# A two-layer diffusion block on one core: seven block products for fourteen more pairs of weight tiles, and modulation steps in three feed-forwards

## The chip, the cores and the metric

The kernel runs on one core of a Trainium2 chip. The metric is the time of one execution on the device in microseconds, the median of several runs.

## The reference

Two layers work on 256 image tokens and 256 context tokens, each a row of 1024 values in float32. A layer is a feed-forward, a token mixer (neighbourhood attention and pooling) and a second feed-forward. In front of each stands an RMS norm with a modulation (shift and scale), behind each a second norm with a gate. The nine modulation vectors of a layer come from a product of a conditioning vector with a 1024 x 9216 matrix, once for the image and once for the context:

```python
def mod_vectors(cvec, w_mod, b_mod):
    m = jax.nn.silu(cvec) @ w_mod + b_mod
    return jnp.split(m, N_MOD, axis=-1)

def swiglu(h, w_gate_up, w_down):
    gate, up = jnp.split(h @ w_gate_up, 2, axis=-1)
    return (jax.nn.silu(gate) * up) @ w_down

def sandwich_ffn(x, w_gate_up, w_down, g_pre, g_post, shift, scale, gate):
    h = modulate(rms_norm(x, g_pre), shift, scale)
    return x + 0.5 * gate * rms_norm(swiglu(h, w_gate_up, w_down), g_post)
```

The hidden width of the feed-forward is 2816, that is 22 tiles of 128. The last layer yields the image tokens only: its vectors 5 to 8 are needed for the image alone, and its second feed-forward runs on 256 tokens.

## The kernel before

**Precision.** Every float32 operand of a matmul is split in a high part (rounded by ScalarE) and a low part (the difference, by VectorE), and `mm3` makes three matmuls of one product. So each weight tile costs ScalarE a copy and VectorE a subtraction ("prep") before TensorE can use it.

**A feed-forward** (`ffn`) goes through 22 pairs of tiles (gate and up) of the first weight. Per pair, `gate_up` makes 2 x 8 products of 512 columns, that is 48 matmuls, and `gate_up_evac` applies SiLU, multiplies and splits the result into G. The pairs form groups; behind each group but the last the down product of the group is made for all tokens in two column halves and added up in Y (copied by ScalarE in the first group, added by VectorE in the later ones). Behind the last group comes the rest of the down product token tile by token tile, and `close` applies norm, gate, residual, next norm and modulation, transposes the tile and splits it into the next input. The four token tiles are 0, 1 (image) and 2, 3 (context). The first pairs ("lead") run on one half of the tokens first, so that they can start before the last two token tiles are closed.

**Seven block products.** For pairs from `LEAD` on of feed-forward (1,0) (layer 1, first), gate and up together form a 2 x 2 block product: gate and up times two halves of the depth, tokens in two halves. `gate_up_seven` makes seven products of quarter size in place of eight: 7 x 4 x 3 = 84 matmuls of 256 columns. It needs sums of weight blocks (`prep_seven`: four GpSimd additions, three and a half weight tiles split) and sums of input blocks (`add_up`, eight additions on GpSimd and eight splits, once per feed-forward), and VectorE adds the products up from PSUM. Its input lies paired: token tiles in the order 2, 0, 3, 1, two and two. Feed-forwards with seven products use `S_GROUPS` (4, 4, 4, 4 and 6 pairs), the others `F_GROUPS` (8, 8 and 6).

**Modulation.** Two vectors of layer 0 are made first by TensorE. The other sixteen are made on VectorE, beside the feed-forwards: a step loads one 128 x 1024 block (`wm`, 512 KB) and multiplies and adds it into an accumulator of each stream (`acc`); after eight such steps a ninth gathers the accumulator with eight small DMAs per stream (`part`), three GpSimd additions, and a matmul with `sel`. These 16 x 9 = 144 steps stand in a list. `fill(n)` takes n more steps from it (fractions add up) after each pair; the rates are `RATE` for (0,0), `LATER` for (0,1), by group. `need` takes what is missing before a vector is read.

**Order of work.** Nothing is issued while the code above runs: a recorder takes the operations down, and `order` plans them by list scheduling, each engine taking the operation that can start first, then by recorded rank (`haste` moves some forward). Buffers come from pools with numbered places: 16 `big`, 2 `raw`, 10 `wk`, 8 PSUM banks. A weight stream (`Stream`) prepares one entry ahead of use. All instructions are issued from one line (387), so the profile's groups go by tile names: `pg`, `pu` gate and up, `p` the seven products, `pd` down, `pt` transposes, `w` and `wb` split weights, `s` sums of weight blocks, `ht` sums of input blocks, `g` and `tt` the pair's result, `c` and `u` the sums of products.

Of the kernel before, what the change touches and what calls it, by code (L numbers as in the profile page):

```python
# [22 lines left out]
NF = 22  # L23
# [3 lines left out]
AHEAD = 1  # L27
F_GROUPS = ((0, 8), (8, 16), (16, 22))
S_GROUPS = ((0, 4), (4, 8), (8, 12), (12, 16), (16, 22))
SEVEN = {(1, 0)}  # L30
NEXT_SEVEN = {(1, 0)}
ORDER = (2, 0, 3, 1)
PLAIN = {t: t for t in range(4)}
PAIRED = {t: i for i, t in enumerate(ORDER)}
# [1 line left out]
LEAD = 3  # L36
# [1 line left out]
BLOCK = 4  # L38
PLACES = {"big": 16, "raw": 2, "wk": 10, "ps": 8, "st": 24}
LIMITS = {"ps": 1}  # L40
RATE = (2.6, 2.6, 2.6)
LATER = (2.6, 4.2, 5.6)
NONE = (0.0,) * 5
BEHIND = 0
MARGIN = 6.0
# [5 lines left out]
XS, CS, ALL = slice(0, S), slice(S, N_TOK), slice(0, N_TOK)  # L51
# [353 lines left out]
def tile_dit_block(  # L405
# [30 lines left out]
    def bank(base="ps"):  # L436
        return rec.tile("ps", [P, 512], F32, base)
# [88 lines left out]
    ws = Stream()  # L526

    def plan_ffn(l, ff):
        groups = S_GROUPS if (l, ff) in SEVEN else F_GROUPS
        for gi, (f0, f1) in enumerate(groups):  # L530
            if l == DEPTH - 1 and ff == 1 and gi == 0:
                for k in range(0, KD, 2):
                    ws.add(wblock[k : k + 2].rearrange("k p c -> p k c"), 2)
                f0 += BLOCK
            for f in range(f0, f1):
                ws.add(wgu[l, ff, f], None, (l, ff) in SEVEN and f >= LEAD)
            f0 = groups[gi][0]
            if gi + 1 < len(groups):
                for h in range(2):
                    for f in range(f0, f1, 4):  # L540
                        ws.add(wdn[l, ff, f : f + 4, :, h * 512 : (h + 1) * 512].rearrange("f p c -> p f c"), 4)
            else:
                for f in range(f0, f1, 2):
                    ws.add(wdn[l, ff, f : f + 2].rearrange("f p c -> p f c"), 2)
# [171 lines left out]
    def fill(n):  # L716

        debt[0] += n
        rec.delay = BEHIND
        while debt[0] >= 1 and todo:  # L720
            steps = todo[0][1]
            steps.pop(0)()
            debt[0] -= 1
            if not steps:
                todo.pop(0)
        rec.delay = 0
# [7 lines left out]
    H = {}  # L734
# [63 lines left out]
    def new_h(paired=False):  # L798
        return Input(paired)
# [89 lines left out]
    def columns(o, w, cs):  # L889
        for k in range(KD):  # L890
            kk = slice(k * P, (k + 1) * P)
            hh = H["now"][k // 4]
            mm3(
                o[:, cs],
                (w[:, 0, kk], w[:, 1, kk]),
                (hh[0][:, k % 4, cs], hh[1][:, k % 4, cs]),
                k == 0,
                k == KD - 1,
            )

    def columns_half(o, w, half):
        for k in range(KD):
            kk = slice(k * P, (k + 1) * P)
            h = H["now"][k // 4][half]
            mm3(
                o[:, half * S : (half + 1) * S],
                (w[:, 0, kk], w[:, 1, kk]),
                (h[:, 0, k % 4, :], h[:, 1, k % 4, :]),
                k == 0,
                k == KD - 1,  # L910
            )
# [21 lines left out]
    def ffn(l, ff, both, nxt, rate, lead, parts):  # L933
        cs = ALL if both else XS
        N = N_TOK if both else S
        seven = (l, ff) in SEVEN
        at = PAIRED if seven else PLAIN
        groups = S_GROUPS if seven else F_GROUPS
        toks = (2, 3, 0, 1) if both else (0, 1)
# [3 lines left out]
        def lhs(f):  # L943
            g = G[f // 2]
            return g[:, f % 2, 0, :], g[:, f % 2, 1, :]
# [6 lines left out]
        def gate_up_evac(f, pg, pu):  # L952
            tt = wtile([P, 2, 512], "tt")
            product(tt[:, :, :N], pg[:, cs], pu[:, cs])
            if f % 2 == 0:
                G[f // 2] = slot([P, 2, 2, N_TOK], "g")
            hi, lo = lhs(f)
            split(hi[:, :N], lo[:, :N], tt[:, 0, :N])

        def gate_up(fs, parts):  # L960
            held = []
            for f in fs:
                held.append((f, ws.get(), ws.get(), bank("pg"), bank("pu")))
            for part in parts:
                for i, (f, wg, wup, pg, pu) in enumerate(held):
                    if seven and part is parts[1] and i == 1:
                        H["now"].add_up()
                    if seven:
                        columns_half(pg, wg, part)
                        columns_half(pu, wup, part)  # L970
                    else:
                        columns(pg, wg, part)
                        columns(pu, wup, part)
                    if part is parts[-1]:
                        gate_up_evac(f, pg, pu)
# [27 lines left out]
        def by_token():  # L1003

            wb = [ws.get() for _ in range(KD)]
            for q in range(BLOCK // 2):
                G[q] = slot([P, 2, 2, N_TOK], "g")
            for t in toks:
                tk = slice(t * P, (t + 1) * P)
                pg, pu = bank("pg"), bank("pu")  # L1010
                for k in range(KD):
                    hh = H["now"][k // 4]
                    for o, c in ((pg, HALVES[0]), (pu, HALVES[1])):
                        mm3(o, (hh[0][:, k % 4, tk], hh[1][:, k % 4, tk]), (wb[k][:, 0, c], wb[k][:, 1, c]), k == 0, k == KD - 1)
                tt = wtile([P, 2, 512], "tt")
                product(tt, pg, pu)
                pt = turn(tt[:, 0, :], 0)
                for q in range(BLOCK // 2):
                    src = pt[:, q * S : (q + 1) * S].rearrange("p (e c) -> p e c", e=2)
                    split(G[q][:, :, 0, tk], G[q][:, :, 1, tk], src)  # L1020

        for gi, (f0, f1) in enumerate(groups):
            f = f0
            if gi == 0 and parts is None:
                by_token()
                f = BLOCK
            elif gi == 0:
                gate_up(tuple(range(lead)), parts)
                f = lead
                fill(lead * rate[gi])  # L1030
            while f < f1:
                if seven:
                    gate_up_seven(f)
                else:
                    gate_up((f,), (cs,))
                f += 1
                fill(rate[gi])
            if gi + 1 < len(groups):
                for h in range(2):
                    hc = slice(h * 512, (h + 1) * 512)  # L1040
                    pd = {t: bank("pd") for t in toks}
                    for q in range(f0, f1, 2):
                        w = ws.get()
                        for i in range(2):
                            hi, lo = lhs(q + i)
                            for t in toks:
                                tk = slice(at[t] * P, (at[t] + 1) * P)
                                c = slice(i * 512, (i + 1) * 512)
                                mm3(
                                    pd[t], (hi[:, tk], lo[:, tk]), (w[:, 0, c], w[:, 1, c]),  # L1050
                                    q + i == f0, q + i == f1 - 1,
                                )
                    for t in toks:
                        if gi == 0:
                            if h == 0 and t % 2 == 0:
                                Y[t // 2] = slot([P, 2, D], "y", F32)
                            nc.scalar.activation(Y[t // 2][:, t % 2, hc], pd[t], AF.Copy)
                        else:
                            nc.vector.tensor_add(Y[t // 2][:, t % 2, hc], Y[t // 2][:, t % 2, hc], pd[t])
# [5 lines left out]
        f0, f1 = groups[-1]  # L1065
        paired = nxt is not None and nxt in NEXT_SEVEN
        toks = ORDER if paired else toks
# [8 lines left out]
        Hn = None  # L1076
        for t in toks:
# [3 lines left out]
            if Hn is None and nxt is not None:  # L1081
                Hn = new_h(paired)
# [4 lines left out]
    def token_mix(l, nxt):  # L1087
        full = l == 0
# [230 lines left out]
        for pr in range(4):  # L1319
            bx = wtile([P, 2, 6, 64], "bx")  # L1320
            nc.sync.dma_start(out=bx, in_=biasx[l, pr])
            now = qk
# [12 lines left out]
                    k_part(qk)  # L1335
                    q_part(qk)

        toks = (2, 3, 0, 1) if full else (0, 1)
        load_gate(l, 5, (0, 1) if full else (0,))
        need(*nxt)  # L1340
        need(nxt[0], nxt[1] + 1)
# [10 lines left out]
        Hn = None  # L1352
        for t in toks:
            if t not in pd:
                pd[t] = (bank("pd"), bank("pd"))
                sweep(pd[t], mixed, w4, t, True, False)
            sweep(pd[t], mixed, kept, t, False, True)
            if Hn is None:
                Hn = new_h()
            close(t, pd[t], None, False, nxt, Hn)  # L1360
        H["now"] = Hn

# [20 lines left out]

    ffn(0, 0, True, (0, 3), RATE, START, (CS, XS))
    token_mix(0, (0, 6))
    ffn(0, 1, True, (1, 0), LATER, LEAD, (CS, XS))
    ffn(1, 0, True, (1, 3), NONE, LEAD, (0, 1))
    token_mix(1, (1, 6))
    ffn(1, 1, False, None, NONE, 0, None)

# [105 lines left out]
```

## Time and profile before

| | us |
|---|---|
| median of 3 runs | 1657.71 |
| lowest and highest | 1657.25, 1659.05 |
| profiled execution | 1658.03 |
| its span, first to last instruction | 1656.0 |

From the matmuls in order of time, the stages of the profiled execution are:

| stage | starts, us |
|---|---|
| feed-forward (0,0) | 37.5 |
| token mixer 0 | 411.8 |
| feed-forward (0,1), pairs 0 to 7 | 603.7 |
| its first down product | 696.8 |
| pairs 8 to 15 | 740.9 |
| second down product | 830.8 |
| pairs 16 to 21 | 875.7 |
| last down product and closing | 943.0 |
| feed-forward (1,0) | 979.9 |
| its first seven-product pair | 1017.7 |
| token mixer 1 | 1328.8 |

Engines: PE is TensorE's matmuls, PEld its weight loads, DVE VectorE, ACT ScalarE, POOL GpSimd, SP the queue that issues the DMAs. A row of the stage view holds the stretch, its length, and the busy time of each engine with its instructions. A row of a tile's view holds the count and the least, median and greatest duration in ns. In a row in order of time, the bracket is the idle time before the instruction and what ended it.

### The profile page before, as it was taken

To read this page: it belongs to the slowest core of one execution; us is meant where nothing else is said; L and a number is where in the kernel's file an instruction comes from. 1 tells how busy PE (TensorE), PEld (TensorE's weight loads), DVE (VectorE), ACT (ScalarE), POOL (GpSimd) and SP (SyncE) were. 2 spreads that over 40 slices of the span, in tenths; PEclk is the share of its full clock that TensorE was granted. 3 is DMA by queue.
4 is the path that set the end of the run, shared out by engine and by line. 5 is a ranking of instruction groups with operands and counts; after the bars stand their busy time and mean duration, and the time that the engine had idled before them with its cause. 6 is when DMAs were issued, how large, how long until landed. Compare 5 with 4: busy or idle time off the path is not lost.

```text
span 1656.0 us, 23501 instructions
## 1 busy us (share of the span) xinstructions
PE 1613.0 (97%) x9074; PEld 1390.3 (84%) x9074; DVE 1212.7 (73%) x1662; ACT 736.6 (44%) x1292; POOL 356.9 (22%) x348
## 2 busy tenths in 40 slices
PE   6999999999999899999999999999999999899998
PEld 4988888888878689888888879999989888778997
DVE  7985766546689779867776488677788778875554
ACT  7522322225566663222222264534444567774442
POOL 1022011101131311110211036363463122210000
PEclk9999999999999999999999999999999999999999
DMA  9466556532221436666698412233233421355551
GB/s 376 185 230 243 209 194 225 175 118 83 86 78 65 157 108 223 235 204 230 211 351 300 159 52 96 83 103 127 77 116 114 144 90 70 132 200 199 196 200 55
DMA packets 98958, 269.09 MB, mean 162 GB/s; under 512 B 9424, under 2 KB 39328, under 8 KB 87072
## 3 DMA queue, kind: packets, MB, share of 16 engines
q1 hardware_dynamic: 98848, 267.60, 45.5%
q8 instruction: 71, 1.16, 0.3%
q14 instruction: 39, 0.32, 0.1%
HBM read 251.80 MB, written 1.09 MB: 153 GB/s over the span
## 4 chain that ended last, share of the span: by engine, by line
PE 84%; DVE 6%; ACT 5%; POOL 2%; issue 2%; DMA 1%; SPq 0%; POOLq 0%; DVEq 0%; ACTq 0%
PE pd_ps L387 26%; PE pu_ps L387 19%; PE pg_ps L387 19%; PE p_ps L387 11%; PE pv_ps L387 2%; ACT n_wk L387 2%; PE pk_ps L387 2%; POOL rs_st L387 2%; DVE w_big L387 1%; PE pq_ps L387 1%; DMA w_big<-in_wmod_dram 1%; PE pt_ps L387 1%; ACT sx_wk L387 1%; PE po_ps L387 1%; ACT w_big L387 1%
## 5 line engine op out<-in xcount | busy, mean ns | idle before, releaser
L387 DVE TENSOR_TENSOR w_big<-raw_raw,w_big 128x1024 fp32r<-128x1024 f32 x293 | 369.8, 1277 | 122.5 <-ACT w_big L387 122.2
L387 PE MATMUL pd_ps<-w_big,g_big 128*128 128x512 f32 x1848 | 430.7, 393 | 0.0
L387 PEld LDWEIGHTS pd_ps<-w_big,g_big 128*128 128x128 f32 x1848 | 345.7, 188 | 77.7 <-ACT grows L387 0.2
L387 ACT ACTIVATE w_big<-raw_raw 128x1024 fp32r<-128x1024 f32 x293 | 302.8, 1054 | 228.9 <-DMA raw_raw<-in_wgu_dram 94.6
L387 PE MATMUL pu_ps<-h_big,w_big 128*128 128x512 f32 (+1 forms) x1944 | 366.4, 341 | 0.0
L387 PEld LDWEIGHTS pu_ps<-h_big,w_big 128*128 128x128 f32 x1944 | 303.7, 188 | 42.5
L387 PE MATMUL pg_ps<-h_big,w_big 128*128 128x512 f32 (+1 forms) x1752 | 330.3, 342 | 1.4 <-ACT h_big L387 1.4
L387 PEld LDWEIGHTS pg_ps<-h_big,w_big 128*128 128x128 f32 x1752 | 275.6, 189 | 41.3 <-ACT h_big L387 1.8
L387 DVE SCALAR_TENSOR_TENSOR acc_wk<-wm_wk,csil,acc_wk 128x1024 f32<-128x1024 f32 x196 | 244.2, 1285 | 81.5 <-DMA wm_wk<-in_wmod_dram 81.2
L387 POOL TENSOR_TENSOR part_wk<-part_wk 128x512 f32<-128x512 f32 (+2 forms) x84 | 87.7, 1045 | 496.1 <-DMA part_wk<-acc_wk 418.5
L387 ACT ACTIVATE g_big<-tt_wk 128x512 fp32r<-128x512 f32 (+1 forms) x84 | 49.2, 586 | 275.6 <-DVE tt_wk L387 258.4
L387 POOL TENSOR_SCALAR rs_st<-sq_st 128x1 f32<-128x1 f32 x24 | 7.5, 312 | 448.8 <-ACT n_wk L387 448.7
L387 POOL TENSOR_TENSOR s_wk<-raw_raw 128x512 f32<-128x512 f32 x38 | 64.1, 1695 | 126.3 <-DMA raw_raw<-in_wgu_dram 120.5
L387 PE MATMUL p_ps<-h_big,w_big 128*128 128x256 f32 x684 | 86.8, 281 | 0.0
L387 PEld LDWEIGHTS p_ps<-h_big,w_big 128*128 128x128 f32 x684 | 83.5, 189 | 0.3
L387 PE MATMUL p_ps<-ht_big,w_big 128*128 128x256 f32 x684 | 82.9, 279 | 0.0
L387 PEld LDWEIGHTS p_ps<-ht_big,w_big 128*128 128x128 f32 x684 | 81.2, 189 | 0.0
L387 DVE TENSOR_TENSOR g_big<-tt_wk,g_big 128x512 fp32r<-128x512 f32 (+1 forms) x84 | 57.8, 688 | 29.3 <-ACT g_big L387 29.2
L387 PE MATMUL pd_ps<-w_big,mix_big 128*128 128x512 f32 x288 | 71.6, 397 | 0.5 <-DVE mix_big L387 0.5
L387 DVE TENSOR_TENSOR w_big<-s_wk,w_big 128x1024 fp32r<-128x1024 f32 x38 | 59.0, 1554 | 15.2 <-ACT w_big L387 15.2
L387 ACT ACTIVATE tt_wk<-pg_ps 128x512 f32<-128x512 f32 (+1 forms) x67 | 35.7, 533 | 75.9 <-PE pg_ps L387 65.8
L387 DVE TENSOR_TENSOR y_big<-y_big,pd_ps 128x512 f32<-128x512 f32 x72 | 48.4, 685 | 27.0 <-PE pd_ps L387 27.0
(157 smaller groups left out, 1771.7 us busy)
## 6 DMA issues: line engine op xcount, KB each, us to landing
raw_raw<-in_wgu_dram SPq DMA_DIRECT2D x84, 1024.0 KB, 4.9
wm_wk<-in_wmod_dram SPq DMA_DIRECT2D x128, 512.0 KB, 6.8
raw_raw<-in_wdn_dram SPq DMA_DIRECT2D x44, 1024.0 KB, 5.2
part_wk<-acc_wk SPq DMA_DIRECT2D x224, 64.0 KB, 2.4
raw_raw<-in_wkq_dram SPq DMA_DIRECT2D x8, 1024.0 KB, 4.8
raw_raw<-in_wout_dram SPq DMA_DIRECT2D x8, 1024.0 KB, 5.0
w_big<-in_wmod_dram SPq DMA_DIRECT2D x7, 1024.0 KB, 16.0
gb_wk<-grow SPq DMA_DIRECT2D x10, 512.0 KB, 6.9
```

Source lines behind the costliest of these rows:

```text
L387: getattr(getattr(nc, op.engine), op.method)(*[self.real(a) for a in op.args], **{k: self.real(a) for k, a in op.kw.items()})
```

## The change

`SEVEN` becomes a table from feed-forward to the first pair that uses seven products: (0,1) from pair 8, (1,0) from pair 3 as before. The input of (0,1) is therefore paired, token mixer 0 closes its tiles in the order 2, 0, 3, 1, `add_up` runs in the lead of (0,1), and (0,1) goes through the five groups of `S_GROUPS`. Its pairs 3 to 7 run as plain products, each in two token halves of 256 columns. The rates of the modulation steps change: more in (0,0), other ones by group in (0,1), and 1.1 a pair in (1,0), which had none.

```diff
-SEVEN = {(1, 0)}
-NEXT_SEVEN = {(1, 0)}
+SEVEN = {(0, 1): 8, (1, 0): 3}
+NEXT_SEVEN = {(0, 6), (1, 0)}
...
-RATE = (2.6, 2.6, 2.6)
-LATER = (2.6, 4.2, 5.6)
+RATE = (2.6, 3.0, 5.0)
+LATER = (4.0, 4.5, 2.0, 1.0, 0.5)
+LAST = (1.1,) * 5
...
-                ws.add(wgu[l, ff, f], None, (l, ff) in SEVEN and f >= LEAD)
+                ws.add(wgu[l, ff, f], None, f >= SEVEN.get((l, ff), NF))
...
-                    if seven and part is parts[1] and i == 1:
+                    if seven and part is parts[1] and i == 1 and H["now"].sums is None:
                         H["now"].add_up()
...
-                if seven:
+                if f >= SEVEN.get((l, ff), NF):
                     gate_up_seven(f)
                 else:
-                    gate_up((f,), (cs,))
+                    gate_up((f,), (0, 1) if seven else (cs,))
...
-        toks = (2, 3, 0, 1) if full else (0, 1)
+        paired = nxt in NEXT_SEVEN
+        toks = (ORDER if paired else (2, 3, 0, 1)) if full else (0, 1)
...
-                Hn = new_h()
+                Hn = new_h(paired)
...
-    ffn(0, 1, True, (1, 0), LATER, LEAD, (CS, XS))
-    ffn(1, 0, True, (1, 3), NONE, LEAD, (0, 1))
+    ffn(0, 1, True, (1, 0), LATER, LEAD, (0, 1))
+    ffn(1, 0, True, (1, 3), LAST, LEAD, (0, 1))
```

## The prediction

> **What bounds the kernel now.** I read the page first (busy shares, then the chain), then the busy time by stage, then TensorE in order of time. The page says that TensorE is the kernel:
>
> ```profile
> span 1656.0 us, 23501 instructions
> PE 1613.0 (97%) x9074; PEld 1390.3 (84%) x9074; DVE 1212.7 (73%) x1662; ACT 736.6 (44%) x1292; POOL 356.9 (22%) x348
> PE 84%; DVE 6%; ACT 5%; POOL 2%; issue 2%; DMA 1%; SPq 0%; POOLq 0%; DVEq 0%; ACTq 0%
> ```
>
> TensorE is busy 97% of the span and 84% of the chain. So removed matmul columns are removed time, as long as the other engines still feed it. The busy time by stage shows where that could fail. In a row stand the stretch, its length, then busy PE, PEld, DVE, ACT, POOL, the granted clock and the DMA share. The first seven rows are the feed-forward (0,1) that is changed; the others are (1,0), which already uses the seven products:
>
> ```profile
> 603.70:640.40 36.70, 36.36 (x305) 35.95 (x305) 33.35 (x41) 19.01 (x34) 6.96 (x9) 1.00 0.36 117
> 640.40:696.80 56.40, 56.40 (x251) 46.01 (x250) 48.68 (x50) 16.43 (x21) 10.47 (x10) 1.00 0.75 279
> 696.80:740.90 44.10, 44.10 (x194) 36.10 (x194) 34.12 (x31) 13.34 (x18) 4.97 (x6) 1.00 0.63 213
> 740.90:830.80 89.90, 89.90 (x400) 73.47 (x398) 63.29 (x66) 21.09 (x30) 17.75 (x18) 1.00 0.61 218
> 830.80:875.70 44.90, 44.90 (x198) 36.52 (x197) 35.66 (x36) 11.28 (x12) 5.82 (x5) 1.00 0.96 336
> 875.70:943.00 67.30, 67.30 (x299) 54.89 (x297) 42.66 (x46) 20.29 (x26) 7.38 (x8) 1.00 0.65 239
> 943.00:979.90 36.90, 35.75 (x163) 28.59 (x163) 22.77 (x39) 16.77 (x41) 6.82 (x11) 1.00 0.18 68
> 979.90:1017.70 37.80, 36.13 (x306) 35.51 (x305) 36.46 (x41) 24.37 (x46) 23.70 (x17) 1.00 0.17 57
> ...
> 1111.20:1150.50 39.30, 39.30 (x337) 39.28 (x336) 30.96 (x35) 18.58 (x24) 12.51 (x7) 1.00 0.27 94
> 1150.50:1172.60 22.10, 22.10 (x99) 18.08 (x98) 17.59 (x19) 6.55 (x8) 15.99 (x10) 1.00 0.34 121
> 1172.60:1212.00 39.40, 39.40 (x337) 39.40 (x336) 31.12 (x35) 18.67 (x24) 12.16 (x7) 1.00 0.28 93
> 1212.00:1234.20 22.20, 22.20 (x99) 18.06 (x98) 18.40 (x19) 6.55 (x8) 16.23 (x10) 1.00 0.35 120
> 1234.20:1293.30 59.10, 59.10 (x505) 59.10 (x504) 49.03 (x55) 26.65 (x36) 21.64 (x12) 1.00 0.34 120
> ```
>
> In all of them TensorE is busy from end to end, but for 1.7 us in the opening of (1,0) and 1.2 us at the end of (0,1). VectorE is next: 75 to 91% up to 740.9, 79 to 83% beside the seven products. That is the cover that the change draws on.
>
> **The change part by part.** *Seven products for pairs 8 to 21.* The rows are TensorE's in order of time: start, length, idle before in brackets.
>
> ```profile
> 808.70 5.68 PE L387 MATMUL pg_ps<-h_big,w_big 128*128 128x512 f32 x24
> ...
> 830.74 0.28 PE L387 MATMUL pm_ps<-sel,part_wk 128*128 128x8 f32 x2
> ...
> 995.31 2.96 PE L387 MATMUL pg_ps<-h_big,w_big 128*128 128x256 f32 x24
> ...
> 1017.69 2.98 PE L387 MATMUL p_ps<-h_big,w_big 128*128 128x256 f32 x24
> ...
> 1234.19 3.01 PE L387 MATMUL p_ps<-h_big,w_big 128*128 128x256 f32 x24
> ...
> 1293.32 23.54 PE L387 MATMUL pd_ps<-w_big,g_big 128*128 128x512 f32 x102
> ```
>
> From 808.70 to 830.74 lie two plain pairs: 22.04 / 2 = 11.02 us each. From 1234.19 to 1293.32 lie six pairs by seven products: 59.13 / 6 = 9.855 us. Fourteen pairs save 14 x 1.165 = **16.3 us**.
>
> *Pairs 3 to 7 in token halves.* Having `seven` set, (0,1) runs them 256 columns wide instead of 512. From 995.31 to 1017.69 lie eight groups of 24 such matmuls, 22.38 / 8 = 2.80 us; a pair is four, 11.19 us, 0.17 over the plain one. Five pairs: **+0.9 us**. Pairs 0 to 2 ran in halves already.
>
> *Five groups instead of three.* The down products are the same in number, so nothing on TensorE. Group 1's sums are now added by VectorE instead of copied by ScalarE; they count below.
>
> *Order 2, 0, 3, 1 out of the token mixer, and `add_up` in the lead.* The opening of (1,0) is what that looks like; that of (0,1) is the present one:
>
> ```profile
> 610.74 0.66 PE L387 MATMUL pt_ps<-ident,n_wk 128*128 128x128 f32 x4 [0.34 <-DVE n_wk L387]
> ...
> 984.20 1.09 PE L387 MATMUL pt_ps<-ident,n_wk 128*128 128x128 f32 x8 [0.20 <-DVE n_wk L387]
> ...
> 990.63 0.66 PE L387 MATMUL pt_ps<-ident,n_wk 128*128 128x128 f32 x4 [0.30 <-ACT n_wk L387]
> ...
> 993.16 0.65 PE L387 MATMUL pt_ps<-ident,n_wk 128*128 128x128 f32 x4 [1.18 <-DVE n_wk L387]
> ```
>
> Idle 0.34 against 0.20 + 0.30 + 1.18 = 1.68 us. Those of (1,0) fall beside the preparation of a first seven-product pair (GpSimd 23.70 us in that row against 6.96), which (0,1) doesn't have there. Bounds 0 and +1.3; I take **+0.7 us**. A matmul queued behind such a transpose waits with it, as TensorE runs in order.
>
> *The modulation steps.* A step is one load and a multiply-add for each stream (a ninth step of each vector gathers). The durations, and the count in the first eight pairs' stretch (603.7 to 740.9):
>
> ```profile
> L387 DVE SCALAR_TENSOR_TENSOR acc_wk<-wm_wk,csil,acc_wk x196: 1270/1280/1567, 46.1 to 915.6; 128x1024 f32<-128x1024 f32 x196
> L387 DVE TENSOR_SCALAR acc_wk<-wm_wk,csil x28: 739/748/1085, 41.1 to 891.2; 128x1024 f32<-128x1024 f32 x28
> ...
> L387 DVE SCALAR_TENSOR_TENSOR acc_wk<-wm_wk,csil,acc_wk 128x1024 f32<-128x1024 f32 x52 | 63.9, 1282 | 16.2 <-DMA wm_wk<-in_wmod_dram 16.2
> L387 DVE TENSOR_SCALAR acc_wk<-wm_wk,csil 128x1024 f32<-128x1024 f32 x6 | 4.2, 749 | 0.0
> ```
>
> All in all 224. By the rates, the first feed-forward now records 8 x 2.6 + 8 x 3.0 + 6 x 5.0 = 74.8 steps (was 57.2), (0,1) to its pair 7 another 4 x 4 + 4 x 4.5 = 34, from pair 8 on 8 + 4 + 3 = 15, and (1,0) the last 21. Layer 1's vectors 5 to 8 need one stream only. In multiply-adds: 132, 60, 14, 18 (sum 224), against 102, 58 and, from 740.9 on, 64. Their small TensorE parts (0.28 us for the two of the row at 830.74) move with them: nothing.
>
> Stage by stage for VectorE. First feed-forward, from its second group on:
>
> ```profile
> 175.10:264.70 89.60, 89.60 (x394) 72.98 (x393) 58.42 (x61) 25.42 (x35) 10.60 (x12) 1.00 0.56 191
> 264.70:308.90 44.20, 44.20 (x193) 36.04 (x192) 33.33 (x31) 9.86 (x10) 4.35 (x4) 1.00 0.57 192
> 308.90:376.20 67.30, 67.30 (x298) 54.97 (x297) 31.99 (x37) 20.36 (x25) 2.32 (x3) 1.00 0.41 146
> ```
>
> 123.7 busy of 201.1; 30 more at 1.28 make 162 (81%): **0**, hidden under TensorE. If that cover went, the price would be the excess over 201 us. Their loads add to a DMA share of 0.41 to 0.57; the 16 gather pieces of a vector wait on SP for the accumulator and hold up the weight loads behind them, as they do now.
>
> The changed one from pair 8 on: the same fourteen pairs of (1,0) take 30.96 + 17.59 + 31.12 + 18.40 + 49.03 = 147 of 182 us; 14 at 1.28 make 165 (91%). (1,0): 18 x 1.28 = 23 us more on shares of 76 to 83%. Bounds for both 0 and +3 us; I take **0**, since no matmul waits for a multiply-add itself.
>
> The tight place is 603.7 to 740.9: VectorE is busy 33.35 + 48.68 + 34.12 = 116.2 of 137.2 already, and gets 2 more multiply-adds (2.6 us), the halves of `add_up` and the group's sums:
>
> ```profile
> L387 DVE TENSOR_TENSOR ht_big<-yg_wk,ht_big x8: 679/689/1796, 1000.4 to 1014.0; 128x512 fp32r<-128x512 f32 x8
> L387 DVE TENSOR_TENSOR w_big<-s_wk,w_big x38: 1215/1226/2406, 1002.1 to 1277.8; 128x1024 fp32r<-128x1024 f32 x38
> ...
> L387 DVE TENSOR_TENSOR y_big<-y_big,pd_ps x72: 674/686/697, 287.7 to 1648.9; 128x512 f32<-128x512 f32 x72
> ```
>
> 8 x 0.69 to 1.8 (say 8 us) and 8 x 0.69 = 5.5. Pair 8's preparation comes in too, three subtractions of 1.23 us: 136 of some 139 us, 98%. A weight split that the planner puts behind a run of ready multiply-adds is then late, and TensorE behind it. Below, 0: multiply-adds may slip past pair 8 at no cost. Above: if VectorE also keeps its present idle 21 us, 136 + 21 - 139 = +18. The nearest row is the opening, VectorE 91% busy with TensorE idle 0.34 us; I take **+2.5 us**.
>
> *GpSimd beside VectorE.* Each new seven-product pair brings four GpSimd additions, which the steps of (0,1) have not met so far:
>
> ```profile
> L387 POOL TENSOR_TENSOR s_wk<-raw_raw x38: 1272/1736/2305, 973.1 to 1260.0; 128x512 f32<-128x512 f32 x38
> ```
>
> A VectorE subtraction of 1.226 us at the median takes up to 2.406 us there, and an addition 1.272 to 2.305. The stage rows of (1,0) hold these lengthenings already, so the sum has no further term for them. [...]
>
> **Sum.** 1658.03 (the profiled execution, span 1656.0 and 2.0 around it; median of the runs 1657.71, so no shift) - 16.3 + 0.9 + 0.7 + 2.5 = **1645.8 us**. About 0.2% (3.3 us) can be told from no change.
>
> **Rivals.**
> 1. *VectorE becomes the bound of the first eight pairs*: weights come late for pairs 4 to 7 and the second group's down product. For it: 98%, and 34 steps of two streams recorded there with no run ahead. Against: before, 58 went through with TensorE idle 0.34 us. With +8 to +18 us: 1651 to 1661, mid 1655. Chance 0.16.
> 2. *Multiply-adds blocked by GpSimd from pair 8 on*: half of the 32 there and in (1,0) pay the 1.18 us between 2.406 and 1.226: 19 us of VectorE. In the changed stage that makes 91% about 95%; where it reaches TensorE 3 to 6 us: 1649 to 1652. Against: (1,0) had such subtractions without TensorE idle. [...] Chance 0.08.
> 3. *Slower: work tiles run short.* Ten `wk` places; a seven-product pair takes six, an accumulator, a weight row and gather pieces now hold two to four. If each of 14 + 19 pairs waits 0.7 us for a place, +23 us gives 1667. It decides from (16.3 - 1.6) / 33 = 0.45 us a pair for no gain. Against: a weight row is read within two multiply-adds, and the 182 us of (1,0) show no wait of TensorE. Chance 0.05.
> 4. *Not what it says*: `SEVEN.get` keyed wrongly would leave plain pairs, 1658 to 1660. The threshold 8 is a group's start and both places that read it agree. Chance 0.02.
>
> **How the numbers follow.** Forecast (VectorE costs 0 to 5 us, 1642 to 1649): 0.69; 1 to 4 as given. Faster by over 0.2% (under 1654.4): 0.69 + 0.08 + half of the first rival 0.08 = 0.85. Within: 0.08 of it less 0.01, plus 0.01: 0.08. Slower (over 1661): 0.07 with the third's 0.05. The range reaches from no stall and slightly cheaper halves, 1641.5, to the middle of the first rival, 1654.
>
> **What would show it.** TensorE: 1176 more seven-product matmuls (14 x 84), pairs of 9.85 us from pair 8 and 11.2 us for 3 to 7; no idle over 1 us between about 640 and 940. Idle at pd, pg or pu with "DVE w_big" as releaser before pair 8 shows the first rival; idle at p with POOL or DVE s_wk behind it the second; waits of GpSimd or ScalarE for freed work tiles, spread over 33 pairs, the third. (0,1) without its lead growing by more than 2 us confirms the order. Wrong is the forecast if pairs cost over 10.2 us, or the first feed-forward lengthens.

## The result and the profile after

The changed kernel takes **1680.67 us** (1679.9 to 1683.23, 4 runs) against 1657.48 (1656.95 to 1659.05, 4 runs): ratio 1.0137, interval 1.0125 to 1.0149. It is slower by 23 us where 12 us less were forecast, far outside the range. The page of its profiled execution (1680.44 us):

```profile
span 1678.7 us, 25309 instructions
PE 1612.6 (96%) x9818; PEld 1423.3 (85%) x9818; DVE 1319.5 (79%) x1770; ACT 767.6 (46%) x1342; POOL 475.8 (28%) x412
PE 66%; DVE 17%; ACT 5%; issue 4%; DMA 4%; SPq 2%; POOL 2%; DVEq 0%; POOLq 0%; ACTq 0%
```

TensorE has 744 matmuls more, as it should: 14 x 84 by seven products in place of 14 x 48, and 5 x 48 by the halves. Of the chain that ended last it held 84%, now 66%; VectorE went from 6 to 17%, DMAs and SP together from 1 to 6%. Where the time lies shows the busy time by stage, first of the kernel before, then of the changed one (stretch, length, busy PE, PEld, DVE, ACT, POOL, granted clock, DMA share); the rows are (0,0), (0,1) and (1,0):

```profile
37.50:411.80 374.30, 374.15 (x1738) 309.48 (x1739) 257.58 (x290) 124.64 (x190) 45.25 (x51) 1.00 0.54 188
...
603.70:979.90 376.20, 374.71 (x1798) 311.53 (x1798) 280.54 (x306) 118.20 (x180) 60.17 (x65) 1.00 0.62 220
979.90:1328.80 348.90, 347.08 (x2446) 323.36 (x2445) 277.57 (x309) 163.67 (x245) 157.69 (x101) 1.00 0.30 105
```

```profile
36.10:417.70 381.60, 377.74 (x1748) 311.89 (x1749) 291.88 (x323) 124.83 (x191) 58.16 (x63) 0.99 0.60 212
...
609.10:994.40 385.30, 366.20 (x2526) 339.20 (x2526) 334.41 (x358) 150.25 (x228) 156.26 (x108) 0.98 0.46 162
994.40:1350.10 355.70, 351.93 (x2453) 326.62 (x2452) 296.58 (x332) 162.51 (x246) 166.34 (x110) 1.00 0.39 134
```

(0,0) lost 7.3 us, (0,1) 9.1 where it should have gained, (1,0) 6.8; mixer 0 and what follows (1,0) stayed within 1.5. TensorE's idle time is length less busy: 19.1 us in (0,1) (before 1.5), 3.9 in (0,0) (0.2), 3.8 in (1,0) (1.8). Besides, the granted clock fell, to 0.99 in (0,0) and 0.98 in (0,1), and TensorE was also busy for longer: in (0,0) 377.74 us with 1748 matmuls, 374.15 with 1738 before.

Now (0,1) in five stretches of the changed kernel: opening, first down product, pairs 4 to 7 with the second one, pairs 8 to 11 with the third one, rest.

```profile
609.10:646.80 37.70, 36.39 (x305) 35.95 (x305) 35.57 (x42) 22.40 (x42) 17.48 (x14) 1.00 0.38 126
646.80:700.00 53.20, 49.07 (x304) 43.91 (x304) 45.44 (x43) 11.78 (x17) 16.32 (x12) 0.94 0.59 212
700.00:757.00 57.00, 55.84 (x384) 51.51 (x382) 52.57 (x52) 15.90 (x20) 18.24 (x12) 1.00 0.58 205
757.00:836.00 79.00, 67.67 (x436) 61.49 (x437) 68.45 (x65) 27.40 (x36) 48.34 (x32) 0.94 0.52 175
836.00:994.40 158.40, 157.25 (x1102) 146.34 (x1102) 132.38 (x159) 72.77 (x114) 55.86 (x40) 1.00 0.37 131
```

The loss sits in two places, 646.8 to 700 (4.1 us idle) and 757 to 836 (11.3 us idle), both with the clock at 0.94. TensorE's rows in order of time name them:

```profile
390.28 15.51 PE L388 MATMUL pd_ps<-w_big,g_big 128*128 128x512 f32 x59 [3.54 <-DVE col L388]
...
673.12 2.50 PE L388 MATMUL pd_ps<-w_big,g_big 128*128 128x512 f32 x5 [4.13 <-DVE g_big L388]
...
757.99 0.39 PE L388 MATMUL pm_ps<-sel,part_wk 128*128 128x8 f32 x2 [2.15 <-POOL part_wk L388]
...
772.76 3.08 PE L388 MATMUL p_ps<-ht_big,w_big 128*128 128x256 f32 x24 [0.91 <-DVE w_big L388]
777.24 1.46 PE L388 MATMUL p_ps<-ht_big,w_big 128*128 128x256 f32 x10 [1.40 <-DVE w_big L388]
...
794.27 4.40 PE L388 MATMUL p_ps<-h_big,w_big 128*128 128x256 f32 x22 [2.52 <-DVE w_big L388]
...
818.20 1.22 PE L388 MATMUL pd_ps<-w_big,g_big 128*128 128x512 f32 x2 [4.05 <-ACT g_big L388]
```

Three ways to be late can be read behind these brackets.

*The wait at 673.12*, in order of time on SP, VectorE and ScalarE (SPq rows are issues, so many of them in so many us):

```profile
650.01 11.02 SPq L388 DMA_DIRECT2D part_wk<-acc_wk  x16
661.12 1.96 SPq L388 DMA_DIRECT2D wm_wk<-in_wmod_dram  x4
661.27 0.63 ACT L388 ACTIVATE g_big<-tt_wk 128x512 fp32r<-128x512 f32 x1 [5.20 <-DVE tt_wk L388]
...
664.88 7.59 DVE L388 SCALAR_TENSOR_TENSOR acc_wk<-wm_wk,csil,acc_wk 128x1024 f32<-128x1024 f32 x6 [3.65 <-DMA wm_wk<-in_wmod_dram]
672.39 0.68 DVE L388 TENSOR_TENSOR g_big<-tt_wk,g_big 128x512 fp32r<-128x512 f32 x1
```

A vector's sixteen gather pieces keep SP issuing for 11.02 us. The modulation blocks queued behind them are issued from 661.12 on, so VectorE stands idle 3.65 us at the head of six multiply-adds, and the split of the last pair's G, whose input ScalarE had ready at 661.9, comes behind all six, at 672.39. TensorE needs it for the down product.

*The waits from 757.99 to 818.20* begin in the same way, then go on by another cause; rows of SP, ScalarE, VectorE and GpSimd:

```profile
746.80 11.33 SPq L388 DMA_DIRECT2D part_wk<-acc_wk  x16
758.24 0.52 SPq L388 DMA_DIRECT2D raw_raw<-in_wgu_dram  x1
763.40 1.06 ACT L388 ACTIVATE w_big<-raw_raw 128x1024 fp32r<-128x1024 f32 x1 [17.07 <-DMA raw_raw<-in_wgu_dram]
...
770.39 2.32 DVE L388 TENSOR_TENSOR w_big<-s_wk,w_big 128x1024 fp32r<-128x1024 f32 x1
771.70 2.15 POOL L388 TENSOR_TENSOR s_wk<-s_wk,raw_raw 128x512 f32<-128x512 f32 x1
772.63 2.30 DVE L388 SCALAR_TENSOR_TENSOR acc_wk<-wm_wk,csil,acc_wk 128x1024 f32<-128x1024 f32 x1
```

Sixteen pieces again, 11.33 us; the next pair's weights are issued only behind them and ScalarE idles 17.07 us. So the preparation of a seven-product pair starts late, and runs with GpSimd's additions and VectorE's subtractions and multiply-adds on top of each other: a subtraction takes 2.32 us in place of 1.23, a multiply-add 2.30 in place of 1.28, and weight tiles are late for `p`.

*The wait at 390.28* in (0,0), rows of SP, ScalarE and VectorE:

```profile
375.81 1.83 SPq L388 DMA_DIRECT2D part_wk<-acc_wk  x3
...
386.70 2.00 ACT L388 ACTIVATE w_big<-raw_raw 128x1024 fp32r<-128x1024 f32 x2 [9.24 <-DMA raw_raw<-in_wv_dram]
387.79 2.36 DVE L388 TENSOR_TENSOR w_big<-raw_raw,w_big 128x1024 fp32r<-128x1024 f32 x2 [9.07 <-ACT w_big L388]
...
390.06 0.17 DVE L388 TENSOR_TENSOR col<-pm_ps,colt 128x16 f32<-128x16 f32 x1
```

The last three of sixteen pieces are issued at 375.81, the loads of the next weights behind them; these land so late that ScalarE and VectorE stand idle for 9 us, and the small addition of a finished vector (`col`), which frees the PSUM bank that the down product needs, queues behind the splits of the late weights.

*The clock* makes the longer waits dearer. Four-us stretches around 673.12, and the one after 794:

```profile
668.00:672.00 4.00, 0.99 (x5) 0.47 (x3) 4.00 (x4) 0.79 (x1) 0.00 (x0) 0.93 1.03 428
672.00:676.00 4.00, 2.88 (x8) 2.42 (x9) 3.57 (x6) 2.31 (x6) 0.00 (x0) 0.50 0.99 414
676.00:680.00 4.00, 4.00 (x14) 3.19 (x14) 4.00 (x6) 0.96 (x2) 0.00 (x0) 0.71 0.80 326
680.00:684.00 4.00, 4.00 (x19) 3.29 (x18) 3.85 (x4) 1.75 (x2) 0.00 (x0) 1.00 0.09 20
...
794.00:798.00 4.00, 3.73 (x18) 3.73 (x19) 4.00 (x7) 1.99 (x4) 0.00 (x0) 0.57 0.39 125
```

After the wait of 4.13 us the granted clock is 0.50, then 0.71, then 1.00: the five matmuls at 673.12 take 0.50 us each where the six pairs' down product (23.54 us for 102) takes 0.23. By an estimate from these rows the slow stretch costs (1 - 0.50) x 2.9 + (1 - 0.71) x 4 = 2.6 us more than the wait itself.

### The profile page after: what moved, and what is told of

It is laid out like the page before. It is cut to its first block, busy times and chain, and to the rows that moved or that the text cites. A ratio compares the mean times of both kernels' runs of the same rounds, so it can differ in the third digit from the quotient of the medians.

```text
span 1678.7 us, 25309 instructions
## 1 busy us (share of the span) xinstructions
PE 1612.6 (96%) x9818; PEld 1423.3 (85%) x9818; DVE 1319.5 (79%) x1770; ACT 767.6 (46%) x1342; POOL 475.8 (28%) x412
## 4 chain that ended last, share of the span: by engine, by line
PE 66%; DVE 17%; ACT 5%; issue 4%; DMA 4%; SPq 2%; POOL 2%; DVEq 0%; POOLq 0%; ACTq 0%
PE pd_ps L388 21%; PE p_ps L388 17%; PE pu_ps L388 10%; PE pg_ps L388 10%; DVE acc_wk L388 5%; DVE w_big L388 4%; SPq L388 2%; DMA wm_wk<-in_wmod_dram 2%; PE pk_ps L388 2%; PE pv_ps L388 2%; ACT n_wk L388 2%; POOL rs_st L388 2%; PE pq_ps L388 1%; DMA w_big<-in_wmod_dram 1%; PE pt_ps L388 1%
## 5 line engine op out<-in xcount | busy, mean ns | idle before, releaser
L388 PE MATMUL pu_ps<-h_big,w_big 128*128 128x256 f32 (+1 forms) x1728 | 288.3, 319 | 0.0
L388 PEld LDWEIGHTS pu_ps<-h_big,w_big 128*128 128x128 f32 x1728 | 248.3, 189 | 23.2
L388 PE MATMUL pg_ps<-h_big,w_big 128*128 128x256 f32 (+1 forms) x1536 | 251.7, 318 | 1.4 <-ACT h_big L388 1.4
L388 PEld LDWEIGHTS pg_ps<-h_big,w_big 128*128 128x128 f32 x1536 | 220.1, 190 | 22.7 <-ACT h_big L388 1.8
L388 POOL TENSOR_TENSOR s_wk<-raw_raw 128x512 f32<-128x512 f32 x66 | 107.1, 1631 | 180.1 <-DMA raw_raw<-in_wgu_dram 105.3
L388 PE MATMUL p_ps<-h_big,w_big 128*128 128x256 f32 x1188 | 152.6, 283 | 2.5 <-DVE w_big L388 2.5
L388 PE MATMUL p_ps<-ht_big,w_big 128*128 128x256 f32 x1188 | 147.5, 282 | 2.3 <-DVE w_big L388 2.3
L388 PEld LDWEIGHTS p_ps<-h_big,w_big 128*128 128x128 f32 x1188 | 146.8, 191 | 3.3 <-DVE w_big L388 2.7
L388 PEld LDWEIGHTS p_ps<-ht_big,w_big 128*128 128x128 f32 x1188 | 143.5, 190 | 2.7 <-DVE w_big L388 2.7
L388 DVE TENSOR_TENSOR w_big<-s_wk,w_big 128x1024 fp32r<-128x1024 f32 x66 | 101.4, 1539 | 7.7 <-ACT w_big L388 7.4
L388 ACT ACTIVATE w_big<-s_wk 128x1024 fp32r<-128x1024 f32 x66 | 69.7, 1057 | 82.6 <-PE pd_ps L388 38.2
```

Source lines behind the costliest of these rows:

```text
L388: getattr(getattr(nc, op.engine), op.method)(*[self.real(a) for a in op.args], **{k: self.real(a) for k, a in op.kw.items()})
```

## The experiments

The theory after this reading: the matmul terms hold; the loss is the modulation steps. The expectations below call it theory A that the steps stand ahead of weight splits and results on SP (the gather pieces) and on VectorE (the multiply-adds; the SP half alone is A1 there), theory B that GpSimd's additions stop VectorE, and theory C that the seven products themselves feed TensorE too slowly. A further rival is that the plan's ranks alone let multiply-adds pass ahead. A stage's length is from the matmuls in order of time; the ratios are to the kernel before, on the same chip.

**Rates alone.** The kernel before with the changed rates and no new seven-product pair:

```diff
-RATE = (2.6, 2.6, 2.6)
-LATER = (2.6, 4.2, 5.6)
+RATE = (2.6, 3.0, 5.0)
+LATER = (4.25, 1.5, 0.5)
+LAST = (1.1,) * 5
...
-    ffn(1, 0, True, (1, 3), NONE, LEAD, (0, 1))
+    ffn(1, 0, True, (1, 3), LAST, LEAD, (0, 1))
```

> The kernel before with the new rates of the modulation steps alone (8 pairs at 4.25, 8 at 1.5, 6 at 0.5 in the feed-forward (0,1); 1.1 a pair in (1,0)), no seven products in (0,1). Theory A (the steps stand ahead of weight splits and pair results on VectorE and SP, and their lateness stops TensorE): the end of the first feed-forward loses its 5.9 us again and (1,0) its 6.8, and (0,1) some too: 1668 to 1675 us. Theory B (GpSimd's additions stop VectorE): there are none in (0,1), so nothing is lost there; 1658 to 1666. Theory C (the seven products of (0,1) cost more than they save): 1657 to 1660.

1682.77 us, ratio 1.0155 (1.0126 to 1.0185); (0,0) 382.9, (0,1) 386.7, (1,0) 352.9. That is more than the 1668 to 1675 of theory A. (0,0) and (1,0) lose 8.6 and 4.0 us, and (0,1) loses 10.5 without one new seven-product pair, so the new rates are enough for a loss. They are not all of it: the next run puts the loss of (0,1) in the changed kernel at 24.5 us, so some 14 us of that come only where the rates and the seven products meet. Its (0,1) from 700 to 745, and the rows behind it (SP, VectorE, GpSimd, TensorE):

```profile
700.00:745.00 45.00, 36.61 (x146) 28.44 (x145) 37.54 (x33) 10.27 (x14) 14.67 (x12) 0.92 0.69 241
```

```profile
699.29 10.18 SPq L388 DMA_DIRECT2D part_wk<-acc_wk  x16
...
705.29 5.17 DVE L388 SCALAR_TENSOR_TENSOR acc_wk<-wm_wk,csil,acc_wk 128x1024 f32<-128x1024 f32 x3
...
706.42 4.35 POOL L388 TENSOR_TENSOR part_wk<-part_wk 128x512 f32<-128x512 f32 x3 [16.13 <-DMA part_wk<-acc_wk]
...
711.91 5.30 PE L388 MATMUL pd_ps<-w_big,g_big 128*128 128x512 f32 x15 [3.18 <-DVE w_big L388]
```

Pieces for 10.18 us, weights late behind them, and multiply-adds of 1.72 us beside GpSimd's additions of the gathered pieces. VectorE is busy 37.5 of 45 us here and only 230 of 387 in the stage, which points to the order within some 50 us and not to the load of the stage.

**No multiply-adds.** The changed kernel without those of steps 1 to 7; loads and gathers stay:

```diff
-    else:
-        nc.vector.scalar_tensor_tensor(out=acc[v], in0=wm, ...)
```

> The changed kernel with the multiply-adds of the modulation left out but for the first of each vector and stream (the loads, the gathers and all the rest stay; the output is that of cut modulations). Theory A, VectorE part: with some 250 us less on VectorE the stalls in (0,1) go; 1643 to 1650. If instead the gathers on SP are what delays the weights: the stalls at weight splits stay, 1655 to 1670. Theory B: the subtractions beside GpSimd are as slow, but VectorE has room; 1645 to 1655. Theory C: 1675 to 1681.

1646.1 us, ratio 0.9934 (0.9911 to 0.9956). Its (0,1):

```profile
604.70:965.40 360.70, 358.21 (x2525) 334.47 (x2525) 253.36 (x292) 152.39 (x228) 146.35 (x108) 1.00 0.51 173
```

360.7 us is 376.2 - 16.3 + 0.9 to a tenth. So the matmul terms of the prediction hold and theory C falls. What lies between 360.7 and 385.2 needs the multiply-adds: 24.5 us, 17.6 of idle and 6.9 of slower clock (366.20 busy less 374.71 - 16.3 + 0.9). (0,0) is 375.9 here. The loads, the gather pieces and GpSimd's additions all still run: without multiply-adds they cost next to nothing. So this run doesn't part theory A from B.

**Steps ranked later.** `BEHIND` puts each step's rank 250 operations back, against the rival of the ranks:

```diff
-BEHIND = 0
+BEHIND = 250
```

> The changed kernel with BEHIND = 250: the steps get a rank 250 operations later in the plan, so that splits and results of about two pairs go first where both are ready. Nothing else changes. Theory A: the waits for g and w in (0,1) shrink; 1650 to 1668. Theories B and C: 1677 to 1684, as the same work stands beside the same work.

1686.87 us, ratio 1.0180 (1.0150 to 1.0209); (0,0) 389.3, (0,1) 384.0. That is above every forecast. A later rank alone is no remedy, so it isn't the plan's ranks by themselves (the prices that the plan goes by are tried further below); why (0,0) grew wasn't followed up.

**No SBUF reads on GpSimd for the seven products.** The four additions of `prep_seven` become constants:

```diff
-nc.gpsimd.tensor_add(s12[:, 0, :], a21, a22)
+nc.gpsimd.memset(s12[:, 0, :], 0.01)
```

> The changed kernel with the four GpSimd additions of each seven-product pair replaced by fills of a constant into the same tiles (which read nothing; the products are then of wrong sums). Theory B: subtractions and multiply-adds of 1.7 to 2.4 us go back to 0.7 to 1.3, and the waits from 770 us on go; 1660 to 1668. Theory A: the wait at 669 us and the one at 387 stay, those at 772 to 821 shrink by a part; 1668 to 1678. Theory C: 1678 to 1682.

1660.18 us, ratio 1.0010 (0.9995 to 1.0025); (0,1) 367.1, (0,0) still 383.0. The group of the sums' subtractions by line, changed kernel and this one (count, busy, mean ns):

```profile
L388 DVE TENSOR_TENSOR w_big<-s_wk,w_big 128x1024 fp32r<-128x1024 f32 x66 | 101.4, 1539 | 7.7 <-ACT w_big L388 7.4
```

```profile
L388 DVE TENSOR_TENSOR w_big<-s_wk,w_big 128x1024 fp32r<-128x1024 f32 x66 | 81.6, 1237 | 27.2 <-ACT w_big L388 26.7
```

From 1539 to 1237 ns, and TensorE's waits of 772 to 821 are gone; that of 4.16 us at the first down product, where no such pair runs, stays. So 18 of the 24.5 us of (0,1) depend on GpSimd's additions. A constant is also written in 0.53 us where an addition takes 1.3 to 2.4, so the sums come sooner as well: how much is the length of the subtractions and how much the earlier sums, this run doesn't part.

**Flat rate in the first feed-forward.** The same 74.8 steps, evenly:

```diff
-RATE = (2.6, 3.0, 5.0)
+RATE = (3.4, 3.4, 3.4)
```

> The changed kernel with the first feed-forward's rates flat, 3.4 a pair in place of 2.6, 3.0, 5.0 (the same 74.8 steps in all). Theory A says that the 7 us of the first feed-forward come from steps crowded in its last six pairs, whose gathers then stand in its last down product (all eight PSUM banks taken, weight loads of the mixer behind the gather pieces on SP): its stage goes from 381.6 back to 374 to 377, the whole to 1673 to 1677. If 30 more multiply-adds cost there wherever they stand: stage 380 to 384, 1679 to 1683.

1680.12 us, ratio 1.0129 (1.0098 to 1.0161); (0,0) 382.5. The crowd in the last six pairs isn't what costs (0,0) its 7 us.

**One copy for the gather.** Eight pieces per stream become one plain copy of the same bytes; the result's order of rows is left out:

```diff
-for q in range(KD):
-    nc.sync.dma_start(out=part[16 * q : 16 * (q + 1)], in_=acc[v][:, q * P : (q + 1) * P])
+nc.sync.dma_start(out=part, in_=acc[v].rearrange("p (q c) -> p q c", q=KD))
```

> The changed kernel with each gather's eight DMAs of 64 KB replaced by one of 512 KB (a plain copy of the accumulator: the transposition over partitions is left out, so the vectors are wrong). SP then issues 28 in place of 224. If SP's blocks of 11 us in front of weight and step loads carry the loss: (0,1) from 385 to 368 to 375, the whole 1660 to 1670. If VectorE's own time carries it: (0,1) stays at 380 to 388, 1675 to 1683.

1667.21 us, ratio 1.0051 (1.0032 to 1.0071); (0,0) 374.0, as before the change, (0,1) 379.8. The time is in the range named for SP's blocks, the stage (0,1) is not: without the many pieces (0,0) is whole, and (0,1) gets back 5.4 of its 24.5 us.

**No loads of modulation blocks.** All steps read one block loaded at the start:

```diff
+wm = wtile([P, D], "wm")
+nc.sync.dma_start(out=wm, in_=wmod[0, 2, 0])
...
-    wm = wtile([P, D], "wm")
-    nc.sync.dma_start(out=wm, in_=wmod[l, j, k])
```

> The changed kernel with the step loads left out: all multiply-adds read one tile loaded at the start (the vectors are wrong), gathers stay. If multiply-adds that wait for their own load (3.65 us at 661 to 665 us) are the main cause: (0,1) 365 to 373 and 1658 to 1668. If VectorE's work and its stops beside GpSimd are: multiply-adds come as early as they are planned and crowd as before, (0,1) 378 to 388, 1673 to 1684.

1676.98 us, ratio 1.0111 (1.0075 to 1.0147): (0,0) 374.4, (0,1) 375.6, but (1,0) 362.9 with a wait of 6.0 us. (0,0) is whole again here too, as it was without multiply-adds: it takes pieces, loads and multiply-adds together to spoil it. (0,1) lies between the two forecasts, and a wait came up in (1,0); this run decides nothing about VectorE's crowding.

**Steps moved away from the second feed-forward**: 82.8 recorded in (0,0), 24.8 in the first eight pairs of (0,1) in place of 34, 10.8 behind:

```diff
-RATE = (2.6, 3.0, 5.0)
-LATER = (4.0, 4.5, 2.0, 1.0, 0.5)
-LAST = (1.1,) * 5
+RATE = (3.0, 4.2, 4.2)
+LATER = (3.1, 3.1, 1.0, 0.8, 0.6)
+LAST = (1.2,) * 5
```

> The changed kernel with steps moved away from (0,1): rates 3.0, 4.2, 4.2 in (0,0) (82.8 steps), 3.1, 3.1, 1.0, 0.8, 0.6 in (0,1) (35.2, was 49), 1.2 in (1,0) (was 1.1). Theory A (VectorE crowded by multiply-adds beside GpSimd's additions and add_up): (0,1) from 385 to 365 to 375, with the first feed-forward at 376 to 383: 1655 to 1670. If only the sum of the steps counts: 1678 to 1684.

1665.64 us, ratio 1.0048 (1.0031 to 1.0066); (0,1) 363.4, (0,0) 392.0. (0,1) gets back 21.8 us. (0,0), for which 376 to 383 was expected, takes half of that, 10.4 us; the runs below have the same rates and 376.8 and 376.9 there, with fewer pieces or with a dearer price for them, so this half hangs on the pieces.

**Gather in two copies through DRAM**, the rows in their order:

```diff
-for q in range(KD): nc.sync.dma_start(out=part[16 * q : 16 * (q + 1)], ...)
+mid = rec.dram(tc.dram_tile([KD, P, P], F32, name=f"mid{l}{j}{v}"), F32, "mid")
+nc.sync.dma_start(out=mid.rearrange("q p c -> p q c"), in_=acc[v].rearrange("p (q c) -> p q c", q=KD))
+nc.sync.dma_start(out=part, in_=mid.rearrange("q (r k) c -> (q r) k c", k=KD))
```

alone, with the moved rates, and with rates in between (2.6, 3.6, 3.6; 3, 3, 1, 1, 1; 1.6):

> The changed kernel with each gather's eight DMAs replaced by two that do the same through DRAM (the accumulator out in one, back in the gathered order in one), 56 issues on SP in place of 224; same vectors, same rates. Theory A1 (the pieces' 0.69 us issues on SP, which the plan takes for 0.45, hold up loads, gathers and the PSUM banks that wait for them): the first feed-forward goes from 381.6 to 374 to 376, (0,1) from 385 to 377 to 382: 1663 to 1670. If only VectorE matters: 1677 to 1683.

> As f1, with the rates of e8 (82.8 steps in (0,0), 35.2 in (0,1), 1.2 a pair in (1,0)). If the two causes (pieces on SP, multiply-adds crowding VectorE in (0,1)) are separate and together account for the loss, the first feed-forward is at 374 to 378, (0,1) at 361 to 365, (1,0) at 351 to 354: 1645 to 1652. If the 392 of e8's first feed-forward was VectorE's own load: 1657 to 1664.

> As f1, with rates 2.6, 3.6, 3.6 in (0,0), 3.0, 3.0, 1, 1, 1 in (0,1) and 1.6 in (1,0), so fewer steps in (0,0) than f2 and more in (1,0). By the two causes: (0,0) 374 to 376, (0,1) 361 to 366, (1,0) 352 to 356: 1645 to 1652, faster than the kernel before by 0.4 to 0.8%. If seven products in (0,1) can't be had beside the steps at all: 1657 or more.

Alone 1666.57 us, ratio 1.0051 (1.0031 to 1.0071), (0,0) 376.5, (0,1) 376.8. With the moved rates 1654.26 us, ratio 0.9977 (0.9966 to 0.9989): faster than the kernel before, but above the 1645 to 1652 expected. Its stages, from an execution of 1651.22 us, are as expected, (0,0) 376.8, (0,1) 363.7, (1,0) 352.7. In between 1664.71, ratio 1.0040 (1.0026 to 1.0055), a plain miss: (0,0) is 375.2 as expected, but (0,1) is 369.2 and (1,0) 357.0, above their ranges. Fewer pieces and fewer steps in the first eight pairs are not enough by themselves; what else held these two stages up wasn't followed up.

**The piece's price in the plan alone.** The planner counts 0.45 us for an issue on SP, and sixteen pieces took 11.02. The same instructions, ordered with 0.69 for a piece:

```diff
-op.cost = 0.45
+op.cost = 0.69 if outs and getattr(outs[0].buf, "name", "") == "part" else 0.45
```

in the changed kernel, with the moved rates, with milder ones (3.0, 4.0, 3.6; 2.8, 2.8, 1.1, 1.0, 0.8; 1.4) and VectorE operations of two wide inputs counted a tenth dearer, and in the kernel before:

> The changed kernel with the plan's price of a gather piece on SP raised from 0.45 to 0.69 us (what the trace shows); the same instructions in another order. If the wrong price is what puts the loads and gathers out of step: first feed-forward 374 to 377, the whole 1665 to 1673. If the issues themselves are the burden, whatever the plan knows: 1675 to 1683.

> The changed kernel with two edits: the plan's price of a piece of the gather (a DMA from the accumulator into part) on SP is 0.69 us, as its sixteen issues in a row took, in place of 0.45; and the rates are those of the run with the steps moved away from the second feed-forward. Two causes that add up (SP's pieces in the first feed-forward, VectorE's crowding in the second): the first feed-forward 375 to 380 us, the second 362 to 366, the time 1648 to 1656 us. One cause only, so that the second edit finds nothing left to take: 1660 to 1666 us, with the first feed-forward above 385 or the second above 370.

> As the run before with milder rates (3.0, 4.0, 3.6 in the first feed-forward, 2.8, 2.8, 1.1, 1.0, 0.8 in the second, 1.4 in the third) and VectorE operations with two wide inputs priced a tenth higher. Two causes that add up: 1648 to 1656 us, the second feed-forward 362 to 368. If the second feed-forward's loss goes by the number of steps in it alone, between the changed kernel's 385 and the 363 of the moved steps by their rates: about 366 to 370, the time 1652 to 1660 us.

> The kernel before with the 0.69 us price of a gather's piece alone. If the price helps only where the steps crowd SP: 1655 to 1660 us, the stages within 2 us of those of before. If the kernel before loses to the same cause: 1640 to 1652 us, with a shorter first or second feed-forward.

The price alone: 1664.49 us, ratio 1.0038 (1.0026 to 1.0050), (0,0) 377.7, (0,1) 373.8: 16 us back with not one instruction changed, only their order. With the moved rates **1649.70 us** (1649.2 to 1650.54, 4 runs), ratio 0.9953 (0.9939 to 0.9968), the best of those that leave nothing out, and inside the range for two causes. Milder: 1654.62, ratio 0.9972 (0.9961 to 0.9984); its (0,1) is as short, 362.5, but (1,0) and what follows are 5 us longer than in the run before, not followed up. In the kernel before: 1659.58, ratio 1.0006 (0.9997 to 1.0016), no gain: there the wrong price did no harm. The best run's stages and one of its gathers:

```profile
36.20:413.10 376.90, 376.10 (x1751) 310.83 (x1752) 311.75 (x335) 124.96 (x190) 73.92 (x69) 1.00 0.62 224
...
607.00:968.70 361.70, 357.51 (x2522) 333.01 (x2521) 310.03 (x337) 150.94 (x228) 153.64 (x102) 1.00 0.44 152
968.70:1320.30 351.60, 349.88 (x2453) 325.52 (x2452) 306.08 (x337) 162.78 (x246) 175.20 (x110) 1.00 0.42 143
```

```profile
651.51 10.18 SPq L388 DMA_DIRECT2D part_wk<-acc_wk  x16
```

The pieces take as long as ever (10.18 us), VectorE is busier in (0,0) than in the changed kernel (312 of 377 us, 83%), and yet TensorE is idle 0.8 us there and 4.2 in (0,1), at full clock. In the whole time the two edits seem to add up: 16.2 us for the price and 15.0 for the moved steps, 31.0 together. By stage they don't (us):

| kernel | (0,0) | (0,1) | (1,0) |
|---|---|---|---|
| changed | 381.6 | 385.2 | 355.7 |
| dearer price | 377.7 | 373.8 | 352.4 |
| moved steps | 392.0 | 363.4 | 352.9 |
| both | 376.9 | 361.7 | 351.6 |

In (0,1) they take 11.4 and 21.8 us off alone, but 23.5 together; in (0,0) the moved steps alone add 10.4, and with the price the stage is shorter than with the price alone. So the agreement of the totals is no sign of two separate causes. What is shown is that (0,1) gets most of its loss back by moved steps, and that (0,0) can take them in once the pieces are priced as measured, or are few.

## Why the prediction was wrong

- *Seven products, -16.3, and halves, +0.9*: right in size, shown by the run without multiply-adds, which is 360.7 us where these terms give 360.8. The rival "not what it says" falls with it.
- *The rival "work tiles run short"*: GpSimd did wait for VectorE to free tiles, 44.2 us in 11 waits of its first additions, where the kernel before had 5.8 us in 2. But the best version waits longer still, 54.5 us, and its (0,1) is 1.0 us over the run without multiply-adds, so this wait alone isn't what costs. By line, GpSimd's first additions in the changed kernel, then in the best one:

```profile
L388 POOL TENSOR_TENSOR s_wk<-raw_raw 128x512 f32<-128x512 f32 x66 | 107.1, 1631 | 180.1 <-DMA raw_raw<-in_wgu_dram 105.3 <-DVE w_big L388 44.2 <-issue 12.8
```

```profile
L388 POOL TENSOR_TENSOR s_wk<-raw_raw 128x512 f32<-128x512 f32 x66 | 115.5, 1758 | 206.9 <-DMA raw_raw<-in_wgu_dram 141.8 <-DVE w_big L388 54.5 <-PE p_ps L388 8.2
```

- *Order and `add_up`, +0.7*: the opening's idle time went from 0.34 to 1.31 us (37.70 - 36.39), within its bounds.
- *First feed-forward, 0, "hidden under TensorE"*: the first failed step. It cost 7.3 us with VectorE at 76% (291.88 of 381.60). The share was the wrong measure: room on VectorE over the stage did not help, since a queue of transfers on SP made a few loads late. The prediction named it ("hold up the weight loads behind them, as they do now") and set nothing for it. The trace of before had the row to price it by: a vector's sixteen pieces took

```profile
663.08 10.18 SPq L387 DMA_DIRECT2D part_wk<-acc_wk  x16
```

  there, and 74.8 steps in place of 57.2 bring two more such vectors into (0,0). A plain copy or only a dearer price there gives 374.0 to 377.7 us. But the pieces alone are not the cause: the stage is whole too without the loads (374.4) or without the multiply-adds (375.9), so it is all three in the order that the plan gave them.
- *VectorE in (0,1), +2.5 for the first eight pairs with a bound of +18, and 0 from pair 8 on with bounds of 0 and +3*: the main failed term. It was 24.5 us. Pair 8 begins at 740.9 in the kernel before and at 758.5 in the changed one. Ahead of it lie 149.4 us in place of 137.2 + 0.9, a loss of some 11 us, within the bound; from it on 235.9 in place of 239.0 - 16.3, a loss of some 13 us, far beyond +3. The step that failed is the reason given for the 0, "no matmul waits for a multiply-add itself": a matmul waits for a split that stands behind multiply-adds in VectorE's order (six in a row took 7.59 us), and from pair 8 on for splits that GpSimd's additions make late and long. The busy shares of 98% and 91% said nothing of either. (The rows for VectorE up to 740.9 give 77 to 91%, not 75 to 91%; nothing hangs on it.)
- *The rivals 1 and 2* named what is there, late weights and multiply-adds of up to 2.30 us in place of 1.28, at 1651 to 1661 and 1649 to 1652. Neither held two further things: that sixteen gather pieces on SP stand at the head of the waits in the rows above, and that with the clock TensorE's busy time grows too, by 6.9 us in (0,1) and 3.6 in (0,0) (377.74 - 374.15). The evidence against them, (1,0) running such pairs without idle time, came from a stage that had no steps at all, so no pieces and no multiply-adds beside GpSimd's additions.
- *GpSimd beside VectorE, no term*: wrong in this place. Beside GpSimd's additions VectorE's instructions took longer: the sums' subtractions 1539 ns on average, 1237 where constants stand in place of the additions, and single multiply-adds 1.72 to 2.30 us in place of 1.28. What in the hardware lengthens them isn't shown. With constants the same number of VectorE instructions is busy 299.1 us in (0,1) in place of 334.4, 35.3 less. The additions went with 18 us of time in (0,1) and only 4 in (1,0), which has more such pairs, 19 against 14; that fits a cost only where VectorE is late anyway.
- *(1,0), 0*: it cost 6.8 us. From 1032 to 1075 of the changed kernel TensorE has 1.97 us idle at a `g` split and a clock of 0.96, 3.7 us together:

```profile
1032.00:1075.00 43.00, 41.03 (x243) 35.97 (x242) 31.61 (x29) 20.28 (x29) 27.33 (x17) 0.96 0.36 124
```

  The rest is spread. The run without multiply-adds has 351.2, so 4.5 of the 6.8 us need these; the best version has 351.6. The 2.3 to 2.7 us over before that both keep are open. Between the best run, 1649.70, and the forecast of 1645.8 lie such remainders: 2.6 us more in (0,0) than before, some 2 in mixer 0, 2.7 in (1,0) and 1.2 behind it, against a (0,1) that is shorter than forecast.

Open, too: within (0,1), the change of SP's pieces or their price, the moved steps and the absence of GpSimd's additions give back 5 to 11, 22 and 18 us, each in a run of its own, which is more together than the 24.5 us there are. The causes work through each other; that each lateness sets off the next fits the rows but isn't shown, and every such run also has a plan of its own, so a clean share for each isn't to be had from these runs.

## What to carry to other kernels

Before costing moved work at nothing because its engine has room in the stage, read the queue that issues its transfers, and count the longest run of issues and of ready instructions that can stand ahead of something TensorE needs. A cost in a planner that was too low by a quarter of a microsecond an issue did no harm here until the work was crowded; measure it from the trace when work is moved. And take evidence that two engines don't disturb each other only from a stage that has both loads.

## What the hardware showed

A long wait of TensorE cost more than itself: after 4.13 us idle the granted clock was 0.50 in the four microseconds in which it went on and 0.71 in the next four. It was also down, to 0.57 at 794, after a single wait of 2.52 us; after the 2.15 us up to 757.99 it was 1.00 from 758 to 762. So in this kernel some waits cost clock and some didn't; from how long on, these rows don't say.

A small DMA held its queue longer than a large one in these rows: sixteen pieces of 64 KB, from SBUF to SBUF, took SP 10.2 to 11.3 us to issue in the rows above, 0.64 to 0.71 each, while four blocks of 512 KB from DRAM took 1.96 us at 661.12, 0.49 each. Four more such blocks, from 667.71 on, are spread over 5.12 us; whether SP waited between them, the row doesn't say.
